# Four instead of three gate groups by seven block products, with their additions in two pieces and all feature-major weights in even chunks

## The chip, the cores and the metric

The kernel runs on one core of a Trainium2 chip. The metric is the device time of one execution in microseconds (us), lower is better. Runs of the kernel before lie between 2510.75 and 2514.31 us, and their median is 2512.1 us. The profile is of one more execution.

## The reference, cut to what matters

Two layers of a decoder trunk are computed for 256 rows (SEQ) of width 2048 (D_MODEL), all in float32:

```
h = rms_norm(x, norm_g[l]);  proj = h @ w_in[l]
(pv, pz, cq, ckv, kr, mz, cb, cc, cx, cz, xq, xz, gpre) = split(proj)
y_pool = pool_mixer(pv) * silu(pz)          # branch 0, width 1024
y_mla  = mla_mixer(cq, ckv, kr) * silu(mz)  # branch 1
y_conv = conv_mixer(cb, cc, cx) * silu(cz)  # branch 2
y_mem  = memory_xattn(xq) * silu(xz)        # branch 3
gates  = sigmoid(gpre + gate_b[l])          # 4 x 2048 columns
merged = sum over b of gates[:, b] * (y_b @ w_branch[l, b])
x = x + merged @ w_out[l]
```

The change concerns `gpre`: 256 rows by 8192 columns with an inner length of 2048, the largest part of the input projection.

## The kernel before, in words

**Products.** Every matrix product is made of TensorE matmuls over tiles of 128 (inner) by 128 by up to 512. To keep float32 accuracy, each operand is split into a high part (`hi`, made by ScalarE with a casting copy) and the rest (`lo`, made by VectorE with a subtraction), and three matmuls are summed: hi·hi, hi·lo, lo·hi. Weights are streamed once from DRAM: `wchunks` (L311) issues a load of 128x1024 numbers on SyncE's queue (`raw`, 4 buffers, L320), then the ScalarE copy (`hi`, 5 buffers, L321) and the VectorE subtraction (`lo`, 5 buffers, L322). Those three are given a priority some instructions ahead of their place (`lead`), so that weights are ready early; how early is limited by the buffers.

**Three ways to multiply.** `tm_block` (L326) makes 256 rows by 512 columns in two PSUM banks: for each of 16 inner tiles and 2 row halves the three matmuls of L334, L335, L336, so 96 matmuls of 512 columns for an inner length of 2048 and 48 for 1024. `fm_block` (L343) and `fine_block` (L372) make feature-major results of 256 or 128 features: one matmul of 512 columns (hi of the weight with hi and lo of the rows side by side) and one of 256 columns (lo of the weight) per inner tile. `seven` (L415) makes 256 rows by 1024 gate columns by the seven products of a fast 2x2 scheme (two row halves by two halves of the inner length, on operand sums `sx` and on weight differences). Per pair of inner tiles it takes two 128x1024 loads (L447), differences on VectorE (L457, L458, L467, L468), splits (L449, L456, L466, L476 on ScalarE, L441 on VectorE), and seven products of three matmuls (L432 to L434): in all 8 x 7 x 3 = 168 matmuls of 512 columns where `tm_block` takes 192.

**PSUM.** There are eight banks: three tiles `acc` of two banks and two tiles `ms` of one. A group of `seven` holds all three `acc` and one `ms` for its whole length. At its end come seven additions that gather the banks (ScalarE copy L485, VectorE L486 to L492), after which the banks are free, then the bias (a load `gb` on SyncE's queue, L496; VectorE L497), the sigmoid on ScalarE (L498) and a store to DRAM (`kept`, L499, on GpSimd's queue).

**How groups are interleaved.** `seven` is a generator: one `next` issues one product. In the stage of the pooling and the convolution branch, whose work is 48 `fine_block`s and 8 small pool matmul blocks per layer, `pull(n)` (L358) first adds n to what is owed and then issues that many products, so that products of the groups stand between the fine blocks on TensorE. A `yield True` ends a pull: in the kernel before there is one, behind the seven additions, so that one fine block stands between the additions and the bias. A fine block has one `ms` bank to itself while a group is open, and the next one needs it back: ScalarE copies it out (`fmt`, L387) and VectorE adds its halves (L388). RATE is (56 x 3 - 8) / 46 = 3.48 products per fine block. `SEVEN` lists three groups per layer: all columns of the pool branch's gates and the first half of the convolution branch's. Their gates are loaded again (`gates`, L971, `g<-kept` on GpSimd's queue) in the gate stages; the other ten blocks of 512 gate columns per layer are made there by `tm_block`.

**Order.** The order of instructions on each engine is set by a scheduler at build time, from the priorities and from the program's order; each engine then runs its list strictly in that order, and SyncE's list of loads as well.

Of the kernel before, what the change touches and what calls it, by code (L numbers as in the profile page):

```python
# [14 lines left out]
ALU = mybir.AluOpType  # L15
AX = mybir.AxisListType

P = 128
AHEAD = 100
NEAR = 40  # L20
PB = 2
D_H, D_MEM, D_LAT, D_XQ, D_MT = 4, 4, 6, 4, 3
SEQUENCE = "A0 A1 F T0 F T1 S0 A2 F V0 T2 S1 A3 F V1 T3 S2 F V2 S3 F V3 X0 X1 F Y0 Y1 X2 X3 F Y2 Y3"
CK = 2
SCRATCH = 1024
FINE = ("pv", "pz", "cc", "cx", "cb", "cz")
D = 2048
S = 256
DEPTH = 2
SEVEN = [(0, 0), (0, 1), (2, 0)]  # L30
RATE = (56 * len(SEVEN) - 8) / 46
KT = D // P
EPS = 1e-6
WINDOWS = (2, 4, 8, 16)
OFF = {
    "pv": 0, "pz": 1024, "cq": 2048, "ckv": 2560, "kr": 3072, "mz": 3136, "cb": 4160,
    "cc": 5184, "cx": 6208, "cz": 7232, "xq": 8256, "xz": 9280, "gate": 10304,
}
# [27 lines left out]
def weight_plan():  # L66
    plan, off = {}, 0

    def add(name, c0, n, nk, kt):
        nonlocal off  # L70
        plan[name, c0] = (off, n, nk, kt)
        off += P * kt * n

    def fm(name):
        if name in FINE:
            for b in range(8):
                add("in", OFF[name] + 128 * b, 128, 8, KT)
        else:
            for b in range(4):
                add("in", OFF[name] + 256 * b, 256, 4, KT)  # L80

    for e in range(4):
        add("mem_kv", 512 * e, 512, 2, KT)
    add("in", OFF["cq"], 512, 2, KT)
    for b in range(2):
        add("in", OFF["ckv"] + 288 * b, 288, 2, KT)
    for b in range(2):
        add("in", OFF["xq"] + 512 * b, 512, 2, KT)
    for hp in range(4):
        add("uq", 384 * hp, 384, 2, 4)  # L90
        add("ukv", 512 * hp, 512, 2, 4)
    for name in ("mz", "xz", "pv", "pz", "cc", "cx", "cb", "cz"):
        fm(name)
    for b in range(2):
        add("pool", 512 * b, 256, 4, 4)
    for bi in range(4):
        for e in range(4):
            if (bi, e // 2) not in SEVEN:
                add("in", OFF["gate"] + bi * D + 512 * e, 512, 2, KT)
            elif e % 2 == 0:  # L100
                add("in", OFF["gate"] + bi * D + 512 * e, 1024, 1, KT)
            add(f"br{bi}", 512 * e, 512, 2, 8)
    for e in range(4):
        add("out", 512 * e, 512, 2, KT)
    return plan, off
# [17 lines left out]
def tile_hybrid_trunk(  # L123
# [3 lines left out]
    V, A, T = nc.vector, nc.scalar, nc.tensor  # L127
# [180 lines left out]
    stream, owed, lead = [], [0.0], [AHEAD]  # L308
# [31 lines left out]
        T.matmul(ps[:, j, :], hi[:, k, n0 : n0 + P], o[:, half].rearrange("p a s -> p (a s)"), start=first, stop=False)  # L340
        T.matmul(ps[:, j, :S], lo[:, k, n0 : n0 + P], o[:, half, 0, :], start=False, stop=last)

    def fm_block(rhs, l, name, c0):  # L343
        ps = acc()
        for k0, nk, kt, n, hi, lo in wchunks(l, name, c0):
            for j in range(2):
                n0 = j * P
                for k in range(nk):
                    o = rhs[(k0 + k) // 2][:, k % 2].rearrange("p a s -> p (a s)")
                    T.matmul(ps[:, j, :], hi[:, k, n0 : n0 + P], o, start=k0 + k == 0, stop=False)  # L350
                for k in range(nk):
                    o = rhs[(k0 + k) // 2][:, k % 2, 0, :]
                    T.matmul(ps[:, j, :S], lo[:, k, n0 : n0 + P], o, start=False, stop=k0 + k == kt - 1)  # L353
        return ps


    def pull(n):
        owed[0] += n  # L358
        while stream and owed[0] >= 1:
            owed[0] -= 1  # L360
            done = next(stream[0], None)
            if done is None:
                stream.pop(0)
            if done:
                break
# [7 lines left out]
    def fine_block(rhs, l, c0):  # L373
        pull(RATE)
        ps = ms()
        for k0, nk, kt, n, hi, lo in wchunks(l, "in", c0):
            for k in range(nk):
                o = rhs[(k0 + k) // 2][:, k % 2].rearrange("p a s -> p (a s)")
                T.matmul(ps, hi[:, k, :], o, start=k0 + k == 0, stop=False)  # L379
            for k in range(nk):  # L380
                o = rhs[(k0 + k) // 2][:, k % 2, 0, :]
                T.matmul(ps[:, :S], lo[:, k, :], o, start=False, stop=k0 + k == kt - 1)  # L382
        return ps

    def fine_sum(dst, ps):
# [29 lines left out]
    def seven(l, bi, ep, h, sx):  # L415
        c0 = bi * D + 1024 * ep
# [3 lines left out]
        left, right = slice(0, 512), slice(512, 1024)  # L420
# [62 lines left out]
        c, u3 = t2("c"), t2("u3")  # L483
# [2 lines left out]
        V.tensor_tensor(g[0][:, 0, :], c, bank[2], ALU.add)  # L486
        V.tensor_tensor(c, c, bank[6], ALU.add)
        V.tensor_tensor(u3, c, bank[7], ALU.add)
        V.tensor_tensor(g[1][:, 1, :], u3, bank[5], ALU.add)
        V.tensor_tensor(c, c, bank[5], ALU.add)  # L490
        V.tensor_tensor(g[1][:, 0, :], c, bank[3], ALU.add)
        V.tensor_tensor(g[0][:, 1, :], u3, bank[4], ALU.subtract)  # L492
        yield True
        for i in range(2):
            gb = tp.tile([P, 512], F32, tag="gb", name=nm("gb"), bufs=2)
# [156 lines left out]
        return kT, vv  # L652

    def silu_half(z, i, h, l, c0):
        ps = fm_block(h, l, "in", c0 + 256 * i)
        sl = slice(2 * i, 2 * i + 2)
        fm_sum(z[:, sl, :], ps)
        sg = t2("sg").rearrange("p (n s) -> p n s", n=2)
        A.activation(sg, z[:, sl, :], AF.Sigmoid)
        V.tensor_tensor(z[:, sl, :], z[:, sl, :], sg, ALU.mult)  # L660
# [502 lines left out]
```

## Time and profile before

| what | value |
|---|---|
| median of 3 runs | 2512.1 us (2510.75 to 2514.31) |
| the profiled execution, time / span | 2505.73 us / 2504.0 us |
| TensorE busy | 2473.0 us, 12258 matmuls |
| VectorE busy / ScalarE busy | 1790.1 us / 1356.9 us |
| pool and convolution stage, layer 0 | 629 to 1031 us |
| pool and convolution stage, layer 1 | 1876 to 2277 us |
| read from HBM | 496.76 MB |

The profile's page gives busy times per engine; a busy time is the union of the instructions' own spans. TensorE's matmuls overlap in time (each row lasts longer than the distance to the next start), so what a matmul costs is read from the distance of starts, or from a count over a stretch. "PE" is TensorE, "DVE" VectorE, "ACT" ScalarE, "SP" SyncE, "POOL" GpSimd. In the view of waits, "A <- B: us, times, longest" says how long A's engine sat idle until B ended the wait. In the view of stretches, each engine has its busy time and the number of its instructions, then the granted TensorE clock, and the share and rate of the DMA engines.

### The profile page before, as it was taken

What the parts mean: (1) busy time and instruction counts of PE and PEld (TensorE: products, weight loads), DVE (VectorE), ACT (ScalarE), POOL (GpSimd) and SP (SyncE); (2) the same over time, 40 slices, a digit from 0 to 9 for tenths busy, and PEclk for the clock granted to TensorE, in tenths of its full rate; (3) what the DMA queues carried; (4) which work ended last, traced back from release to release, by engine and by line L of the source; (5) the groups of instructions that cost most, each with busy time, mean ns of one, the idle gap of its engine ahead of it and who ended that gap; (6) DMA issues with size and microseconds to landing.
All of it is one profiled execution on the core that took longest, in us unless ns stands there. A gap on an engine that the chain in (4) does not pass through costs nothing.

```text
span 2504.0 us, 33197 instructions
## 1 busy us (share of the span) xinstructions
PE 2473.0 (99%) x12258; PEld 2080.0 (83%) x12258; DVE 1790.1 (71%) x2646; ACT 1356.9 (54%) x1881; POOL 40.4 (2%) x88
## 2 busy tenths in 40 slices
PE   8999999999999999999999999999999999999999
PEld 7888888888887888888888888888888878888887
DVE  6766787555898888766474677875558888888653
ACT  7556674444565555445454566744445655555442
POOL 0000000000000000100000000000000000001000
PEclk9999999999999999999999999999999999999999
DMA  8664436677555666886655654366766556668764
GB/s 315 218 205 160 149 127 211 213 237 234 185 198 198 201 217 204 299 291 231 219 186 163 205 164 148 124 219 219 225 222 209 193 191 199 217 217 307 246 228 144
DMA packets 154052, 522.03 MB, mean 208 GB/s; under 512 B 17312, under 2 KB 18336, under 8 KB 153888
## 3 DMA queue, kind: packets, MB, share of 16 engines
q1 hardware_dynamic: 142800, 481.06, 58.2%
q0 software_dynamic: 10368, 37.75, 4.2%
q8 instruction: 96, 1.57, 0.3%
q10 hardware_dynamic: 720, 1.09, 0.1%
q14 instruction: 68, 0.56, 0.1%
HBM read 496.76 MB, written 23.07 MB: 208 GB/s over the span
## 4 chain that ended last, share of the span: by engine, by line
PE 84%; DVE 7%; DMA 5%; ACT 2%; issue 1%; SPq 0%; DVEq 0%; ACTq 0%
PE acc L336 18%; PE acc L335 18%; PE acc L334 18%; PE ms L379 10%; DMA raw<-in_weights_dram 5%; PE ms L382 5%; PE acc L350 4%; PE acc L353 2%; DVE lo L322 2%; PE acc L433 2%; PE acc L432 2%; PE acc L434 2%; DVE lo L441 1%; ACT hi L321 1%; PE ms L873 1%
## 5 line engine op out<-in xcount | busy, mean ns | idle before, releaser
L322 DVE TENSOR_TENSOR lo<-raw,hi 128x1024 fp32r<-128x1024 f32 (+1 forms) x788 | 943.3, 1199 | 578.3 <-ACT hi L321 576.1
L321 ACT CAST hi<-raw 128x1024 fp32r<-128x1024 f32 (+1 forms) x788 | 813.1, 1033 | 900.0 <-PE acc L336 568.0
L334 PE MATMUL acc<-hi,op 128*128 128x512 f32 (+2 forms) x2112 | 812.6, 385 | 5.8 <-ACT op L558 5.8
L335 PE MATMUL acc<-lo,op 128*128 128x512 f32 (+2 forms) x2112 | 808.4, 383 | 1.9 <-DVE lo L322 1.8
L336 PE MATMUL acc<-hi,op 128*128 128x512 f32 (+2 forms) x2112 | 808.9, 383 | 0.0
L334 PEld LDWEIGHTS acc<-hi,op 128*128 128x128 f32 x2112 | 397.1, 188 | 79.4 <-ACT op L558 6.4
L335 PEld LDWEIGHTS acc<-lo,op 128*128 128x128 f32 x2112 | 397.2, 188 | 77.3 <-DVE lo L322 3.5
L336 PEld LDWEIGHTS acc<-hi,op 128*128 128x128 f32 x2112 | 396.8, 188 | 76.9 <-issue 1.3
L379 PE MATMUL ms<-op,hi 128*128 128x512 f32 x1536 | 384.9, 392 | 6.7 <-ACT fmt L387 4.8
L379 PEld LDWEIGHTS ms<-op,hi 128*128 128x128 f32 x1536 | 280.8, 188 | 68.2 <-ACT fmt L387 12.3
L441 DVE TENSOR_TENSOR lo<-raw,hi 128x512 fp32r<-128x512 f32 x192 | 206.3, 1088 | 28.2 <-ACT hi L449 12.8
L382 PEld LDWEIGHTS ms<-op,lo 128*128 128x128 f32 x1536 | 209.5, 190 | 15.0
L382 PE MATMUL ms<-op,lo 128*128 128x256 f32 x1536 | 214.1, 282 | 0.0
L350 PE MATMUL acc<-op,hi 128*128 128x512 f32 x512 | 144.3, 397 | 0.0
L350 PEld LDWEIGHTS acc<-op,hi 128*128 128x128 f32 x512 | 87.6, 189 | 11.7 <-issue 0.7
L353 PEld LDWEIGHTS acc<-op,lo 128*128 128x128 f32 x512 | 78.5, 189 | 10.7 <-issue 0.7
L353 PE MATMUL acc<-op,lo 128*128 128x256 f32 x512 | 83.8, 283 | 0.0
L433 PE MATMUL acc<-lo,sx 128*128 128x512 f32 x192 | 76.4, 398 | 6.5 <-DVE lo L441 6.5
L432 PE MATMUL acc<-hi,sx 128*128 128x512 f32 x192 | 75.5, 393 | 1.0 <-ACT hi L476 1.0
L434 PE MATMUL acc<-hi,sx 128*128 128x512 f32 x192 | 74.8, 390 | 0.0
L387 ACT COPY fmt<-ms 128x512 f32<-128x512 f32 x112 | 65.0, 580 | 6.3 <-PE ms L382 5.9
L456 ACT CAST hi<-raw 128x1024 fp32r<-128x1024 f32 x48 | 50.4, 1051 | 33.1 <-DMA raw<-in_weights_dram 15.4
(254 smaller groups left out, 1985.4 us busy)
## 6 DMA issues: line engine op xcount, KB each, us to landing
raw<-in_weights_dram SPq DMA_DIRECT2D x836, 512.0 KB, 4.3
sums<-g POOLq DMA_DIRECT2D x24, 512.0 KB, 4.5
mg<-sums POOLq DMA_DIRECT2D x24, 512.0 KB, 8.1
raw<-in_weights_dram SPq DMA_DIRECT2D x32, 288.0 KB, 2.8
gb<-in_gate_b_dram SPq DMA_DIRECT2D x32, 256.0 KB, 4.4
raw<-in_weights_dram SPq DMA_DIRECT2D x16, 384.0 KB, 3.0
kept<-g POOLq DMA_DIRECT2D x12, 512.0 KB, 6.5
g<-kept POOLq DMA_DIRECT2D x12, 512.0 KB, 6.6
```

What stands on the lines that cost most here:

```text
L321: A.copy(hi[:, :m], raw[:, :m])
L322: V.tensor_tensor(lo[:, :m], raw[:, :m], hi[:, :m].bitcast(F32), ALU.subtract)
L334: T.matmul(ps[:, t, :n], hh, hi[:, k, :], start=kk == 0, stop=False)
L335: T.matmul(ps[:, t, :n], hh, lo[:, k, :], start=False, stop=False)
L336: T.matmul(ps[:, t, :n], hl, hi[:, k, :], start=False, stop=kk == kt - 1)
L350: T.matmul(ps[:, j, :], hi[:, k, n0 : n0 + P], o, start=k0 + k == 0, stop=False)
L353: T.matmul(ps[:, j, :S], lo[:, k, n0 : n0 + P], o, start=False, stop=k0 + k == kt - 1)
L379: T.matmul(ps, hi[:, k, :], o, start=k0 + k == 0, stop=False)
L382: T.matmul(ps[:, :S], lo[:, k, :], o, start=False, stop=k0 + k == kt - 1)
L432: T.matmul(bank[i], lh[0], hi[:, cols], start=u == 0, stop=False)
L433: T.matmul(bank[i], lh[0], lo[:, cols], start=False, stop=False)
L441: V.tensor_tensor(x[1][:, cols], raw[:, cols], x[0][:, cols].bitcast(F32), ALU.subtract)
```

## The change

Four things change together:

- `SEVEN` gets a fourth group, `(2, 1)`: the second half of the convolution branch's gates is made in the pool and convolution stage, too, and the two blocks of `tm_block` for it in the last gate stage go. `RATE` becomes (56 x 4 - 8) / 44 = 4.91.
- `pull` issues at most `MOST` = 6 products.
- The additions of a group come in two pieces with a `yield True` after each: first the four that fill `g[0]` and free the `ms` bank, then the three for `g[1]`. Two fine blocks (or small pool blocks) stand between the last product and the bias.
- `mz` and `xz` are packed as `pv`, `pz` and the others were: eight blocks of 128 columns in chunks of 8 inner tiles by 128 columns, where it was four blocks of 256 columns in chunks of 4 by 256. `fm_block` runs one feature tile after the other. Loads have the same size and number.

```
-SEVEN = [(0, 0), (0, 1), (2, 0)]
-RATE = (56 * len(SEVEN) - 8) / 46
+SEVEN = [(0, 0), (0, 1), (2, 0), (2, 1)]
+RATE = (56 * len(SEVEN) - 8) / 44
+MOST = 6
...
     def pull(n):
         owed[0] += n
-        while stream and owed[0] >= 1:
+        left = MOST
+        while stream and owed[0] >= 1 and left:
             owed[0] -= 1
+            left -= 1
...
         V.tensor_tensor(u3, c, bank[7], ALU.add)
+        V.tensor_tensor(g[0][:, 1, :], u3, bank[4], ALU.subtract)
+        yield True
         V.tensor_tensor(g[1][:, 1, :], u3, bank[5], ALU.add)
         V.tensor_tensor(c, c, bank[5], ALU.add)
         V.tensor_tensor(g[1][:, 0, :], c, bank[3], ALU.add)
-        V.tensor_tensor(g[0][:, 1, :], u3, bank[4], ALU.subtract)
         yield True
...
+    def fm_run(ps, rhs, l, c0):
+        for k0, nk, kt, n, hi, lo in wchunks(l, "in", c0):
+            for k in range(nk):
                o = rhs[(k0 + k) // 2][:, k % 2].rearrange("p a s -> p (a s)")
                T.matmul(ps, hi[:, k, :], o, start=k0 + k == 0, stop=False)
            for k in range(nk):
                o = rhs[(k0 + k) // 2][:, k % 2, 0, :]
                T.matmul(ps[:, :S], lo[:, k, :], o, start=False, stop=k0 + k == kt - 1)
...
+    def fm_block(rhs, l, c0):
+        ps = acc()
+        for j in range(2):
+            fm_run(ps[:, j, :], rhs, l, c0 + P * j)
+        return ps
```

**TensorE at the end of the first group, layer 0.** Before, the group's last product (into the bank `ms1064`) is followed by a whole fine block (`ms1298`, 32 matmuls, of which the rows that differ only in the inner tile are printed together):

```order
L432 MATMUL ms1064_5746<-hi1292_6876,op154_788 128x512
L433 MATMUL ms1064_5746<-lo1293_6877,op154_788 128x512
L434 MATMUL ms1064_5746<-hi1292_6876,op154_788 128x512
L379 MATMUL ms1298_6898<-op110_573,hi1300_6900 128x512 x2
L379 MATMUL ms1298_6898<-op124_632,hi1300_6900 128x512 x2
L379 MATMUL ms1298_6898<-op129_658,hi1300_6900 128x512 x2
```

Now the same product stands among the small pool blocks (`ms1257`, `ms1263`, four matmuls each), and the next group's first matmul (`acc1275`) comes right behind the second of them (rows that repeat are left out):

```order
L425 MATMUL ms1064_5748<-hi1255_6687,op154_790 128x512
L336 MATMUL ms1257_6694<-op1082_5833,hi1252_6681 128x512
L337 MATMUL ms1257_6694<-op1082_5833,lo1253_6682 128x256
L426 MATMUL ms1064_5748<-lo1256_6688,op154_790 128x512
L427 MATMUL ms1064_5748<-hi1255_6687,op154_790 128x512
L336 MATMUL ms1263_6714<-op1082_5833,hi1252_6681 128x512
L337 MATMUL ms1263_6714<-op1082_5833,lo1253_6682 128x256
L425 MATMUL acc1275_6763<-hi1281_6771,op110_575 128x512
```

The end of the first group has moved from between two fine blocks into the small pool blocks of the branch's first half. The second and third group's ends are followed by two fine blocks in a row, the fourth's by the stage's last two.

**SyncE's list of loads at the same place.** Before, the bias loads of the second group (`gb1549`, `gb1550`) stand behind the weights of that group's first pair of inner tiles (`raw1319`, `raw1320`) and one fine block's (`raw1340`, `raw1343`), and ahead of the second pair's:

```order
L447 DMA raw1319_6978<-in_weights_dram 128x1024
L447 DMA raw1320_6979<-in_weights_dram 128x1024
L320 DMA raw1340_7057<-in_weights_dram 128x1024
L320 DMA raw1343_7079<-in_weights_dram 128x1024
L496 DMA gb1549_8189<-in_gate_b_dram 128x512
L496 DMA gb1550_8194<-in_gate_b_dram 128x512
L447 DMA raw1347_7107<-in_weights_dram 128x1024
L447 DMA raw1348_7108<-in_weights_dram 128x1024
```

Now the second pair's weights stand ahead of them, and a fine block's behind:

```order
L440 DMA raw1279_6767<-in_weights_dram 128x1024
L440 DMA raw1280_6768<-in_weights_dram 128x1024
L316 DMA raw1288_6800<-in_weights_dram 128x1024
L316 DMA raw1291_6822<-in_weights_dram 128x1024
L440 DMA raw1297_6860<-in_weights_dram 128x1024
L440 DMA raw1298_6861<-in_weights_dram 128x1024
L490 DMA gb1479_7789<-in_gate_b_dram 128x512
L490 DMA gb1480_7794<-in_gate_b_dram 128x512
L316 DMA raw1304_6881<-in_weights_dram 128x1024
```

The bias loads still stand among the next group's weights, and now three times per layer, one pair of weight loads later than before.

More of the change, by code (lines that the diff above doesn't have):

```diff
@@ L25 @@
 SCRATCH = 1024
-FINE = ("pv", "pz", "cc", "cx", "cb", "cz")
 D = 2048
@@ L74, in fm @@
     def fm(name):
[L75 to L80, printed above, removed]
+        for b in range(8):
+            add("in", OFF[name] + 128 * b, 128, 8, KT)
     for e in range(4):
@@ L341, in fm_tile @@
         T.matmul(ps[:, j, :S], lo[:, k, n0 : n0 + P], o[:, half, 0, :], start=False, stop=last)
-    def fm_block(rhs, l, name, c0):
-        ps = acc()
[L345 to L353, printed above, removed]
+    def fm_run(ps, rhs, l, c0):
+        for k0, nk, kt, n, hi, lo in wchunks(l, "in", c0):
+            for k in range(nk):
+                o = rhs[(k0 + k) // 2][:, k % 2].rearrange("p a s -> p (a s)")
+                T.matmul(ps, hi[:, k, :], o, start=k0 + k == 0, stop=False)
+            for k in range(nk):
+                o = rhs[(k0 + k) // 2][:, k % 2, 0, :]
+                T.matmul(ps[:, :S], lo[:, k, :], o, start=False, stop=k0 + k == kt - 1)
+    def fm_block(rhs, l, c0):
+        ps = acc()
+        for j in range(2):
+            fm_run(ps[:, j, :], rhs, l, c0 + P * j)
         return ps
@@ L375, in fine_block @@
         ps = ms()
[L376 to L382, printed above, removed]
+        fm_run(ps, rhs, l, c0)
         return ps
@@ L654, in silu_half @@
     def silu_half(z, i, h, l, c0):
-        ps = fm_block(h, l, "in", c0 + 256 * i)
+        ps = fm_block(h, l, c0 + 256 * i)
         sl = slice(2 * i, 2 * i + 2)
```

## The prediction

> **What bounds the kernel now.** I read the page first. TensorE is busy in 99% of the span; VectorE, which makes the low parts of all weights, in 71%.
>
> ```profile
> span 2504.0 us, 33197 instructions
> PE 2473.0 (99%) x12258; PEld 2080.0 (83%) x12258; DVE 1790.1 (71%) x2646; ACT 1356.9 (54%) x1881; POOL 40.4 (2%) x88
> ```
>
> An average hides the stages, so I asked next for four stretches: the pool and convolution stage of layer 0, what follows it, a stretch of the gate stage of layer 1, and the pool and convolution stage of layer 1.
>
> ```profile
> core 0: us, PE busy (x) PEld busy (x) DVE busy (x) ACT busy (x) POOL busy (x), PEclk, DMA share, GB/s
> 629.00:1031.00 402.00, 392.94 (x2075) 334.21 (x2074) 348.94 (x447) 232.33 (x275) 4.83 (x13) 1.00 0.62 205
> 1031.00:1119.00 88.00, 87.39 (x395) 72.04 (x394) 59.67 (x57) 37.78 (x41) 9.14 (x17) 1.00 0.86 317
> 1660.00:1860.00 200.00, 200.00 (x884) 165.65 (x883) 107.19 (x89) 83.66 (x80) 5.51 (x11) 1.00 0.71 228
> 1876.00:2277.00 401.00, 392.75 (x2073) 334.17 (x2072) 348.28 (x445) 233.34 (x275) 4.84 (x13) 1.00 0.62 205
> ```
>
> In the gate stage TensorE never waits and VectorE is half idle (107 of 200 us). In the stage where the groups are interleaved it is the other way: VectorE is busy 348.9 of 402 us (0.868), and TensorE is idle for 402.0 - 392.9 = 9.1 us in layer 0 and 8.2 us in layer 1. The change moves work from the first kind of stage into the second. What TensorE waits for there, in layer 0:
>
> ```profile
> engine line waited for: us in total, times, longest us
> PE acc L433 <- DVE lo L441: 3.3, 3, 1.6
> PE ms L379 <- ACT fmt L387: 2.6, 4, 1.4
> PE ms L379 <- ACT hi L321: 1.4, 1, 1.4
> PE ms L340 <- ACT fmt L387: 1.2, 1, 1.2
> ```
>
> The rest is one wait of a product for ScalarE. Two kinds stand out: a product waits for the low part of its weights (L433), and a fine or small block waits for the one `ms` bank, which ScalarE has still to copy out (`fmt`). So TensorE's matmuls set the time, and the change is worth what it takes off them less what it adds to these waits.
>
> **The change part by part, for one layer.**
>
> *Gate blocks that go.* Two `tm_block`s of 96 matmuls leave the last gate stage. The gate stretch above holds 884 matmuls in 200 us without a wait, 0.2262 us each: 192 x 0.2262 = **-43.4 us**. Their 32 low parts, bias and sigmoid go with them, all hidden there.
>
> *The fourth group.* One pull of TensorE's list in layer 0, between two fine blocks:
>
> ```profile
> 839.80 1.11 PE L382 MATMUL ms<-op,lo 128*128 128x256 f32 x8
> ...
> 842.59 1.11 PE L382 MATMUL ms<-op,lo 128*128 128x256 f32 x8
> 843.55 0.40 PE L432 MATMUL ms<-hi,op 128*128 128x512 f32 x1
> ...
> 845.61 1.98 PE L379 MATMUL ms<-op,hi 128*128 128x512 f32 x8
> ```
>
> Nine product matmuls start from 843.55 to 845.61: 0.229 us each, 0.69 us a product. The group has 168: **+38.5 us**. (One chunk of a fine block, eight `lo` and eight `hi`, takes 842.59 - 839.80 = 2.79 us, a fine block 5.58.)
>
> *Even chunks.* The count of matmuls stays. In the old form, four `lo` take as long as two `hi`:
>
> ```profile
> 353.53 0.63 PE L350 MATMUL acc<-op,hi 128*128 128x512 f32 x2
> 354.00 0.63 PE L353 MATMUL acc<-op,lo 128*128 128x256 f32 x4
> 354.47 0.40 PE L350 MATMUL acc<-op,hi 128*128 128x512 f32 x1
> ```
>
> So four and four take 0.94 + 0.47 = 1.41 us, eight and eight 2.82 against 2.79. A layer has 32 of these; 0.03 x 32 = 1.0 is the most, and the last digit could make it nothing. I take **-0.5 us** (0 to -1.0). A low part is now wanted after eight matmuls, not four, which can only relax a wait.
>
> *VectorE in the stage.* These rows are of the same stage, with the mean duration behind the busy time; below them VectorE's own list at the first group's end:
>
> ```profile
> L322 DVE TENSOR_TENSOR lo<-raw,hi 128x1024 fp32r<-128x1024 f32 x100 | 121.9, 1222 | 38.3 <-ACT hi L321 37.7
> L467 DVE TENSOR_TENSOR raw<-raw,raw 128x512 f32<-128x512 f32 x24 | 16.5, 687 | 0.2
> ```
>
> ```profile
> 757.16 0.68 DVE L457 TENSOR_TENSOR raw<-raw 128x512 f32<-128x512 f32 x1
> 757.76 0.68 DVE L487 TENSOR_TENSOR c<-c,acc 128x512 f32<-128x512 f32 x1
> ...
> 763.42 1.22 DVE L497 TENSOR_TENSOR g<-g,gb 128x1024 f32<-128x1024 f32 x1
> 764.56 0.69 DVE L669 TENSOR_TENSOR z<-z,sg 128x512 f32<-128x512 f32 x1
> ```
>
> Starts lie 0.60 us apart behind an operation of 512 columns and 1.14 behind one of 1024. A group has 24 whole low parts, 8 half ones, 32 differences, 7 additions and 2 bias additions: 26 x 1.14 + 47 x 0.60 = 57.8 us, against 38.5 us that it gives TensorE. VectorE's work in the stage becomes 348.9 + 57.8 = 406.7 us, TensorE's 392.9 + 38.5 = 431.4. TensorE stays the longer, and its bare time is what counts, but VectorE's slack falls from 44 to 25 us. [...]
>
> *The limit of six products* only moves products to later pulls; no cost of its own.
>
> *The additions in two pieces, and the waits.* Where TensorE stood still, with the wait and its releaser in brackets:
>
> ```profile
> 724.44 0.50 PE L340 MATMUL ms<-op,hi 128*128 128x512 f32 x1 [1.16 <-ACT fmt L387]
> ...
> 768.17 0.50 PE L433 MATMUL acc<-lo,sx 128*128 128x512 f32 x1 [1.60 <-DVE lo L441]
> ...
> 771.62 0.50 PE L433 MATMUL acc<-lo,sx 128*128 128x512 f32 x1 [1.09 <-DVE lo L441]
> ...
> 913.78 2.11 PE L379 MATMUL ms<-op,hi 128*128 128x512 f32 x8 [1.38 <-ACT hi L321]
> ```
>
> 724 is the first small pool block while a group is open; 768 and 772 lie behind the first group's additions, 914 behind the second's. The view of waits over the whole span has both layers' waits of the first kind, and the longer one:
>
> ```profile
> PE ms L340 <- ACT fmt L387: 3.1, 2, 2.0
> ```
>
> Four things change. The small blocks of both halves of the pool branch now meet an open group's `ms` bank right behind a fine block: a second wait of the 724 kind, +1.2 to +2.0, taken +1.6. The first group's end has about 2.8 us of small blocks beside it (four, each of two matmuls of 0.229 and two of 0.12, an eighth of 843.55 - 842.59) where a fine block gave 5.58; its additions must free `acc` first: -1 to +4, taken +0.5, since the waits at 768 and 772 that it replaces fall away. A third end between groups is added, at the price of the 914 row: +1.4 (0 to 2.7). And pulls of five or six products last 3.4 to 4.1 us where three last 2.1, so ScalarE's copy of the `ms` bank is no longer late: of the 2.6 us, -2.0 (0 to -2.6). Together **+1.5 us**; the bounds, -1 to +5, are narrower than the sum of the ends since these waits share VectorE's backlog.
>
> *Behind the stage.* Six blocks of 48 branch matmuls in a row become eight, with gates and sums reloaded beside the weights. In 1031 to 1119 the DMA engines are busy 0.86 of the time and TensorE lost 88.00 - 87.39 = 0.6 us. The two added blocks want less (no sum is stored there): **+0.3 us** (0 to 0.8).
>
> Sum per layer: -43.4 + 38.5 - 0.5 + 1.5 + 0.3 = -3.6; twice, **-7.2 us**. The profiled execution (2505.73 us, 1.7 around its span) would be at 2498.5; it stands 6.4 below the runs' median, to which I apply the same sum: **2504.9 us**.
>
> [...]
>
> **The rivals.**
>
> *VectorE sets the pace (slower).* The busiest 100 us that I found for it:
>
> ```profile
> 660.00:760.00 100.00, 98.34 (x521) 83.95 (x520) 90.00 (x120) 60.85 (x74) 0.13 (x1) 1.00 0.57 195
> ```
>
> If 0.90 is all that it can hold, since it also waits for ScalarE's casts (37.7 us in the L322 row), the stage takes 406.7 / 0.90 = 451.9 us, +49.9: per layer -43.4 + 49.9 - 0.5 + 0.3 = +6.3, in all 2524.7. It decides from where the share cannot pass 406.7 / 445.6 = 0.913 (402.0 + 43.4 + 0.5 - 0.3 = 445.6). My forecast needs 406.7 / 442 = 0.92, more than any row shows. Against it: what holds back the casts in this stage is largely TensorE, which has not yet released the buffers:
>
> ```profile
> ACT hi L321 <- PE ms L379: 45.2, 34, 1.7
> ```
>
> The supply thus has some 45 us of room, and the group takes 57.8 - 38.5 = 19.3 of it. Chance 0.17.
>
> *The bias loads hold up the weights (no change).* SyncE's list at the first group's end:
>
> ```profile
> 752.50 3.12 SPq L320 DMA_DIRECT2D raw<-in_weights_dram  x2
> 764.67 2.07 SPq L496 DMA_DIRECT2D gb<-in_gate_b_dram  x2
> 768.18 3.74 SPq L447 DMA_DIRECT2D raw<-in_weights_dram  x2
> ```
>
> SyncE stands for 9.0 us until the first bias addition (763.42 + 1.22) frees a `gb` buffer, and the weights queued behind, for fine blocks and for products, come late. The second piece puts the bias one block later still, up to 5.58 us. If each of three ends then costs the two product waits that followed here (1.60 and 1.09, 2.7), where one does today, that is +5.4 in place of +1.5: per layer +0.3, in all 2512.7. For it: the row. Against: one more pair of weights now stands ahead of the bias loads. Chance 0.20.
>
> *The waits go (faster than forecast).* If two fine blocks beside the additions and the longer pulls remove all but about 4 us of the 9.1 us idle, that is -5.0 in place of +1.5: per layer -10.1, in all 2491.9. Against it: the first group's end has small blocks beside it. Chance 0.15.
>
> *That the fourth group is not interleaved* is excluded: 47 pulls of 4.91 and 8 of 1 make 239 steps, four groups need 4 x 58 = 232, and in TensorE's new list the last product stands ahead of the stage's last two fine blocks.
>
> **How the numbers follow.** The forecast's own case has 0.48; by its waits it reaches from 2 x (-43.4 + 38.5 - 0.5 - 1 + 0.3) = -12.2 to -0.2, so 2499.9 to 2511.9. A change under 0.2% (5.0 us) is about what a measurement of this kernel cannot tell from none. Faster by more: the waits go, 0.15, some three quarters of the forecast's case, 0.37, and 0.02 of the bias loads; 0.54. Within: 0.11 of the forecast and 0.16 of the bias loads; 0.27. Slower: VectorE 0.17 and 0.02 of the bias loads; 0.19. The range leaves out about half of the case in which the waits go and most of VectorE's: 2493 to 2519.
>
> **What would show it.** In the changed profile, the pool and convolution stage should last about 442 us with VectorE busy about 407; the gate stage behind it should be shorter by 43 us; waits for `fmt` ahead of fine blocks should be fewer and those of products at group ends should show VectorE's `lo`. The prediction is wrong if the stage exceeds 446 us, or if TensorE's idle time in it falls under 5 us.

## The result, and the profile after

The changed kernel takes 2538.51 us (median of 4 runs, 2536.42 to 2539.46) where the kernel before takes 2511.69 us beside it (4 runs): a ratio of 1.0115, with a 95% interval of 1.0103 to 1.0127. It is slower, and outside the predicted range. The profiled execution took 2536.42 us, its span 2534.1 us, 30.1 more than before. (The medians lie 26.8 us apart; the profiled execution of the kernel before, 2505.73 us, was shorter than its other runs.)

The page of the changed kernel: TensorE is busy 8.0 us longer than before although it runs 48 matmuls fewer, in a span that is 30.1 us longer, and VectorE is busy 75.8 us longer.

```profile
span 2534.1 us, 33322 instructions
PE 2481.0 (98%) x12210; PEld 2080.2 (82%) x12210; DVE 1865.9 (74%) x2756; ACT 1379.8 (54%) x1915; POOL 44.6 (2%) x96
```

The lengths of the stages, read as the distance from each stage's first matmul to the next one's (the third row up to the first matmul behind the stage's last fine block):

| stage | before | after | forecast per layer |
|---|---|---|---|
| attention, layer 0 and 1 | 160.0, 160.0 | 159.0, 159.0 | -0.5 with the next row |
| gate blocks behind it | 255.7, 255.7 | 256.2, 256.2 | |
| pool and convolution, layer 0 and 1 | 401.8, 401.0 | 461.5, 460.8 | +40.0 |
| what follows, to the next attention or the end | 429.0, 227.1 | 383.6, 182.3 | -43.1 |

The loss is all in one stage: 59.7 us more per layer where 40.0 were forecast. Of these, 1.2 us are not a loss: in the changed kernel five matmuls of the next stage's first gate block (L330 to L332) run ahead of the stage's last fine block, and the fourth row is shorter by as much.

```profile
1085.50 0.40 PE L330 MATMUL acc<-hi,op 128*128 128x512 f32 x1
...
1086.43 0.39 PE L331 MATMUL acc<-lo,op 128*128 128x512 f32 x1
1086.66 1.98 PE L343 MATMUL ms<-op,hi 128*128 128x512 f32 x8
```

These are the stretches of the changed kernel: the pool and convolution stage of both layers, then what follows the first, and the first 80 us of it alone. The columns are those of the prediction's stretches.

```profile
630.70:1092.20 461.50, 440.99 (x2246) 370.80 (x2245) 410.36 (x522) 262.74 (x310) 5.89 (x15) 0.98 0.61 201
1891.00:2351.80 460.80, 440.99 (x2247) 371.12 (x2246) 410.21 (x522) 263.10 (x310) 5.89 (x15) 0.98 0.61 201
1092.20:1475.80 383.60, 383.60 (x1837) 323.13 (x1836) 239.66 (x355) 200.72 (x312) 10.23 (x19) 1.00 0.68 229
1092.20:1172.00 79.80, 79.80 (x362) 66.06 (x361) 56.69 (x53) 35.31 (x38) 10.23 (x19) 1.00 0.96 360
```

VectorE is busy 410.4 us, the forecast's 407. TensorE is idle for 461.5 - 441.0 = 20.5 us where it was 9.1, and its busy time is 441.0 where 392.9 + 38.5 = 431.4 was forecast. The granted clock, 1.00 before, has fallen to 0.98. The DMA engines move 201 GB/s here, and 360 GB/s in the 80 us behind the stage, so the transfers themselves are not at their limit. TensorE's waits in the stage of layer 0:

```profile
PE ms L343 <- ACT fmt L380: 6.9, 8, 1.5
PE ms L336 <- ACT fmt L380: 3.5, 3, 2.1
PE acc L425 <- DVE c L480: 3.1, 1, 3.1
PE acc L426 <- DVE lo L434: 2.7, 3, 1.5
PE ms L343 <- ACT hi L317: 1.3, 3, 0.4
```

Against the rows of before, the waits for the copy out of the `ms` bank (`fmt`) have grown from 2.6 + 1.2 to 6.9 + 3.5 us, where I had let them shrink. The wait for VectorE's `c` is the first group's end among the small pool blocks. ScalarE, which makes those copies and the high parts, waits in this stage of the changed kernel for:

```profile
ACT hi L317 <- DMA raw<-in_weights_dram: 51.3, 44, 4.4
ACT hi L469 <- DVE raw L461: 32.1, 15, 5.9
ACT hi L449 <- DMA raw<-in_weights_dram: 25.1, 17, 2.1
ACT hi L459 <- DVE raw L451: 14.4, 11, 3.4
ACT hi L317 <- PE ms L343: 13.1, 11, 1.7
ACT hi L442 <- DMA raw<-in_weights_dram: 12.9, 15, 2.2
```

And in the same stage of the kernel before, which the prediction did not quote except for the second row:

```profile
ACT hi L321 <- DMA raw<-in_weights_dram: 54.8, 37, 4.0
ACT hi L321 <- PE ms L379: 45.2, 34, 1.7
ACT hi L449 <- DMA raw<-in_weights_dram: 14.2, 11, 2.1
ACT hi L456 <- DMA raw<-in_weights_dram: 7.6, 7, 2.2
ACT hi L476 <- DVE raw L468: 6.4, 5, 2.8
ACT hi L466 <- DVE raw L458: 4.1, 3, 1.5
```

The room, casts that wait for TensorE, has gone from 45.2 to 13.1 us, and casts now wait for loads for 89.3 us (51.3 + 25.1 + 12.9). They had already waited 76.6 us for loads before (54.8 + 14.2 + 7.6). What grew most is another wait: casts that wait for VectorE's differences of the weights, from 10.5 us (6.4 + 4.1) to 46.5 (32.1 + 14.4). One wait for a load and what came of it, first ScalarE's list of the changed kernel, then SyncE's, VectorE's and TensorE's:

```profile
1015.34 0.61 ACT L442 CAST hi<-raw 128x512 fp32r<-128x512 f32 x1
1020.28 1.04 ACT L317 CAST hi<-raw 128x1024 fp32r<-128x1024 f32 x1 [4.33 <-DMA raw<-in_weights_dram]
1021.23 0.58 ACT L380 COPY fmt<-ms 128x512 f32<-128x512 f32 x1
```

```profile
1015.43 7.51 SPq L316 DMA_DIRECT2D raw<-in_weights_dram  x3
```

```profile
1014.19 1.22 DVE L434 TENSOR_TENSOR lo<-raw,hi 128x1024 fp32r<-128x1024 f32 x1
```

```profile
1015.22 1.12 PE L346 MATMUL ms<-op,lo 128*128 128x256 f32 x8
1016.17 0.40 PE L425 MATMUL acc<-hi,op 128*128 128x512 f32 x1
...
1020.05 0.39 PE L427 MATMUL acc<-hi,op 128*128 128x512 f32 x1
1021.87 2.11 PE L343 MATMUL ms<-op,hi 128*128 128x512 f32 x8 [1.43 <-ACT fmt L380]
```

Read it backwards. TensorE waits 1.43 us for the `ms` bank. The fine block in that bank ended at about 1016.2, six products ago, but its copy (`fmt`, 1021.23) stands in ScalarE's list behind a cast that waits 4.33 us for its load. SyncE issued that load at 1015.43, just when VectorE's low part ended (1014.19 + 1.22 = 1015.41) and with it the use of a `raw` buffer. So a buffer that came free late made a load late, the load a cast, and the cast a copy that had nothing to do with it.

### The profile page after: what moved, and what is told of

Same layout as the page of the kernel before. It is cut to its first block, busy times and chain, and to the rows that moved or that the text cites. A ratio compares the mean times of both kernels' runs of the same rounds, so it can differ in the third digit from the quotient of the medians.

```text
span 2534.1 us, 33322 instructions
## 1 busy us (share of the span) xinstructions
PE 2481.0 (98%) x12210; PEld 2080.2 (82%) x12210; DVE 1865.9 (74%) x2756; ACT 1379.8 (54%) x1915; POOL 44.6 (2%) x96
## 5 line engine op out<-in xcount | busy, mean ns | idle before, releaser
L318 DVE TENSOR_TENSOR lo<-raw,hi 128x1024 fp32r<-128x1024 f32 (+2 forms) x756 | 903.1, 1197 | 525.2 <-ACT hi L317 523.4
L317 ACT CAST hi<-raw 128x1024 fp32r<-128x1024 f32 (+2 forms) x756 | 777.6, 1032 | 785.4 <-PE acc L332 527.4
L330 PE MATMUL acc<-hi,op 128*128 128x512 f32 (+2 forms) x1984 | 763.9, 385 | 6.0 <-ACT op L552 5.7
L331 PE MATMUL acc<-lo,op 128*128 128x512 f32 (+2 forms) x1984 | 758.9, 382 | 1.4 <-DVE lo L318 1.3
L332 PE MATMUL acc<-hi,op 128*128 128x512 f32 (+2 forms) x1984 | 759.1, 383 | 0.0
L330 PEld LDWEIGHTS acc<-hi,op 128*128 128x128 f32 x1984 | 373.3, 188 | 75.7 <-ACT op L552 6.4
L331 PEld LDWEIGHTS acc<-lo,op 128*128 128x128 f32 x1984 | 373.5, 188 | 71.7 <-DVE lo L318 2.5
L332 PEld LDWEIGHTS acc<-hi,op 128*128 128x128 f32 x1984 | 373.0, 188 | 71.3 <-DVE op L553 0.7
L343 PE MATMUL ms<-op,hi 128*128 128x512 f32 x1536 | 390.7, 396 | 17.0 <-ACT fmt L380 13.6
L343 PEld LDWEIGHTS ms<-op,hi 128*128 128x128 f32 x1536 | 283.0, 190 | 81.5 <-ACT fmt L380 21.0
L434 DVE TENSOR_TENSOR lo<-raw,hi 128x1024 fp32r<-128x1024 f32 (+1 forms) x256 | 274.6, 1087 | 32.6 <-ACT hi L469 15.5
L346 PEld LDWEIGHTS ms<-op,lo 128*128 128x128 f32 x1536 | 210.5, 191 | 15.4
L343 PE MATMUL acc<-op,hi 128*128 128x512 f32 x512 | 134.9, 397 | 0.0
L426 PE MATMUL acc<-lo,sx 128*128 128x512 f32 x256 | 102.4, 400 | 6.0 <-DVE lo L434 5.7
L449 ACT CAST hi<-raw 128x1024 fp32r<-128x1024 f32 x64 | 67.3, 1052 | 71.4 <-DMA raw<-in_weights_dram 56.9
L425 PE MATMUL acc<-hi,sx 128*128 128x512 f32 x256 | 101.6, 397 | 4.1 <-ACT hi L459 2.5
L469 ACT CAST hi<-raw 128x1024 fp32r<-128x1024 f32 x64 | 67.2, 1051 | 67.4 <-DVE raw L461 61.4
L343 PEld LDWEIGHTS acc<-op,hi 128*128 128x128 f32 x512 | 90.6, 189 | 16.2 <-issue 1.3
L427 PE MATMUL acc<-hi,sx 128*128 128x512 f32 x256 | 100.7, 394 | 0.0
L459 ACT CAST hi<-raw 128x1024 fp32r<-128x1024 f32 x64 | 67.2, 1050 | 37.1 <-DVE raw L451 26.1
```

The costliest lines, as they stand in the source:

```text
L317: A.copy(hi[:, :m], raw[:, :m])
L318: V.tensor_tensor(lo[:, :m], raw[:, :m], hi[:, :m].bitcast(F32), ALU.subtract)
L330: T.matmul(ps[:, t, :n], hh, hi[:, k, :], start=kk == 0, stop=False)
L331: T.matmul(ps[:, t, :n], hh, lo[:, k, :], start=False, stop=False)
L332: T.matmul(ps[:, t, :n], hl, hi[:, k, :], start=False, stop=kk == kt - 1)
L425: T.matmul(bank[i], lh[0], hi[:, cols], start=u == 0, stop=False)
```

## The experiments

The theories at the start: VectorE's work sets the pace (theory A in the expectations); the four `raw` buffers do not free themselves fast enough for two streams of weights (theory B); the first group's end among the small blocks halves the clock (theory C); the bias loads hold up the weights. In the table, "stage" is the pool and convolution stage of layer 0 and 1, and the ratio is to the kernel before on the same chip. The stages of e3, e4, e6, e7 and e10 contain 1.2 us of the next stage as well, that of e8 0.5 us. e6, e13 and e15 leave out a part of the computation.

| kernel | time, us | ratio, 95% interval | stage, us |
|---|---|---|---|
| e1_chunks | 2504.85 | 0.9993 (0.9983 to 1.0002) | 401.5, 401.9 |
| e2_four_plain | 2532.46 | 1.0101 (1.0086 to 1.0116) | 458.7, 455.9 |
| e3_pieces | 2515.57 | 1.0032 (1.0020 to 1.0045) | 407.4, 408.4 |
| e8_one_piece | 2537.08 | 1.0120 (1.0105 to 1.0135) | 461.3, 460.7 |
| e4_raw5 | 2495.88 | 0.9956 (0.9942 to 0.9971) | 442.1, 440.7 |
| e5_early | 2530.54 | 1.0089 (1.0071 to 1.0107) | 457.3, 460.1 |
| e6_relief | 2522.07 | 1.0061 (1.0037 to 1.0084) | 456.2, 455.5 |
| e7_bias_pool | 2533.33 | 1.0108 (1.0090 to 1.0126) | 461.8, 459.6 |
| e9_three_raw5 | 2488.57 | 0.9929 (0.9915 to 0.9942) | 392.8, 393.5 |
| e10_trims | 2535.83 | 1.0117 (1.0101 to 1.0134) | 457.5, 458.4 |
| e11_raw5_early | 2491.53 | 0.9939 (0.9927 to 0.9952) | 441.0, 439.2 |
| e12_plain_raw5 | 2498.26 | 0.9967 (0.9954 to 0.9979) | 440.3, 441.4 |
| e13_raw5_early_relief | 2482.36 | 0.9898 (0.9884 to 0.9913) | 434.6, 434.8 |
| e14_three_raw5_chunks | 2488.78 | 0.9921 (0.9906 to 0.9935) | 392.9, 393.8 |
| e15_three_raw5_relief | 2489.97 | 0.9929 (0.9912 to 0.9945) | 393.3, 393.1 |
| e16_bias_add_pool | 2501.22 | 0.9966 (0.9955 to 0.9976) | 441.9, 445.5 |
| e17_three_raw5_again | 2488.58 | 0.9921 (0.9900 to 0.9942) | 393.9, 393.5 |

### Which part of the change loses

**The even chunks alone** (before, with `fm_run` and eight blocks of 128 columns).

> The kernel before with the even chunks alone, three groups. All theories: the attention stage, which takes 160.0 us per layer before, should lose about 1 us as it does with the whole change (159.0), so 2509 to 2512 us, and the pool and convolution stage should stay at 401 to 402 us. If the chunks were to blame for the loss, this would be slower by several us.

Attention is 1.0 us shorter per layer, the gate blocks behind it 0.5 longer: -0.5 as forecast, and no difference that the measurement can tell.

**The fourth group alone** (before, with one list entry; `RATE` follows).

```
-SEVEN = [(0, 0), (0, 1), (2, 0)]
+SEVEN = [(0, 0), (0, 1), (2, 0), (2, 1)]
```

> The kernel before with the fourth group alone: RATE is (56 x 4 - 8) / 46 = 4.70, the additions are in one piece, there is no limit of six products, and the chunks are the old ones. Theory A, VectorE's work sets the pace: its work is the same as with the whole change, the stage is again 455 to 462 us, 2532 to 2540 us in all. Theory B, weights come late because the groups hold the four raw buffers, and ScalarE's copies of the fine block's bank stand in line behind the casts: also 450 to 460 us. Theory C, the first group's end among the small pool blocks and the halved clock behind it make the loss: here the first group ends just behind the pool blocks with one fine block beside it, so no long wait and no stretch of half clock there; the stage is about 445 us and the total about 2510 us.

1.0101 of the 1.0115: the fourth group makes nearly the whole loss by itself. Its first end lies elsewhere, and the stage still takes 458.7 us where theory C expected 445, so where that end stands is not the main cause. (Stretches of half clock, shown in the last section, are not gone here: 6.8 us in layer 0 and 10.2 in layer 1, against 17.0 per layer in the whole change; the mean granted clock of the profiled execution is 0.996 here and 0.992 there. e5 below tests theory C more closely.)

**The two pieces alone** (before with the additions in two pieces and `/ 44`, three groups) **and the change with one piece**.

> The kernel before with the additions in two pieces and RATE (56 x 3 - 8) / 44 = 3.64, three groups. Theories A and B: VectorE's work and the loads are as before, so the time stays within 5 us of before (2507 to 2517 us). Theory C: the second piece leaves a wait at the first group's end among small pool blocks, 3 to 8 us per layer, more if the clock is halved behind it: 2518 to 2530 us.

> The changed kernel with the additions in one piece again, RATE 4.91, limit six, four groups. The first group still ends among the small pool blocks, one pull earlier done. Theories A and B: within 5 us of the changed kernel (2533 to 2543 us). Theory C: the waits at the ends change; if the second piece is to blame, 2515 to 2530 us.

With three groups the two pieces, with the rate that belongs to them, cost 8.5 us over the kernel before beside it (0.3%): more than the 5 us that theories A and B allow, so they have some cost of their own. With four, taking them back gains nothing (1.0120 against 1.0115).

### What the stage waits for

**A fifth `raw` buffer in the changed kernel.** Its 4 KB per partition are taken from temporaries:

```
-            raw = wp.tile([P, 1024], F32, tag="raw", name=nm("raw"), bufs=4)
+            raw = wp.tile([P, 1024], F32, tag="raw", name=nm("raw"), bufs=5)
...
-            pT = tp.tile([P, 512], F32, tag="pT", name=nm("pT"), bufs=2)
+            pT = tp.tile([P, 384], F32, tag="pT", name=nm("pT"), bufs=2)
...
-        return tp.tile([P, 512], F32, tag="t2", name=nm(s), bufs=7)
+        return tp.tile([P, 512], F32, tag="t2", name=nm(s), bufs=6)
```

(and two kinds of small tiles from 6 to 4 buffers).

> The changed kernel with five raw buffers in place of four, paid for with one t2 buffer, a narrower pT, and four small buffers in place of six. Theory A, VectorE's work sets the pace: the stage shortens by at most 3 us per layer from 461. Theory B, late weights in the four raw buffers hold up ScalarE's list: weights come earlier, ScalarE's waits for loads in the stage (about 90 us per layer) fall by a third or more, and the stage shortens by 8 us or more per layer. Theory C: the long wait at the first group's end stays, the stage is shorter by under 5 us.

The stage falls by 19.4 and 20.1 us, with VectorE's work where it was. These are its stretches, TensorE's waits and ScalarE's in layer 0:

```profile
629.40:1071.50 442.10, 433.91 (x2247) 369.76 (x2246) 408.29 (x522) 261.79 (x310) 5.89 (x15) 0.99 0.64 210
```

```profile
PE ms L336 <- ACT fmt L380: 2.8, 2, 2.5
PE acc L425 <- DVE c L480: 2.3, 1, 2.3
PE acc L426 <- DVE lo L434: 1.4, 1, 1.4
```

```profile
ACT hi L459 <- DVE raw L451: 35.2, 16, 3.5
ACT hi L317 <- PE ms L343: 33.8, 26, 2.1
ACT hi L469 <- DVE raw L461: 23.3, 8, 4.8
ACT hi L317 <- DMA raw<-in_weights_dram: 13.3, 11, 2.4
```

The waits of fine blocks (`L343`) for `fmt` are gone; ScalarE's waits of this kind (L317) for loads fell from 51.3 to 13.3 us, and its waits for TensorE rose from 13.1 to 33.8: the room is back. With the loads of the groups (L449, L442) its waits for loads fell from 89.3 to 18.9 us.

**The control: the same temporaries cut, `raw` at four.**

> The changed kernel with the smaller t2, pT and small pools alone, and four raw buffers: the control for the run with five. Theory B: no gain, 2533 to 2545 us. If the scheduler's new order under other pools, and not the fifth buffer, made the gain, it is near 2496 us.

1.0117, as without the cut. (Its profiled execution, 2529.93 us, was one of its shorter ones, with stages of 457.5 and 458.4 us.) Against that profile the fifth buffer still takes 15.4 and 17.7 us off the stage.

**The first end moved** (the owed count starts one pull higher).

```
-        owed[0] = -RATE
+        owed[0] = RATE
```

> The changed kernel with what is owed starting at +RATE in place of -RATE: the first group ends in the last two fine blocks ahead of the first half's small pool blocks, not among them. Theory C: the wait of 3 us and the 10 us of half clock behind it go, 8 to 12 us per layer, so 2514 to 2524 us. Theories A and B: the work of the stage is the same, what is saved there is lost elsewhere: 2530 to 2542 us.

The half clock falls from 17.0 to 3.4 and 6.8 us per layer (the mean granted clock of the profiled execution is 0.998 against 0.992), and the stage hardly moves (457.3, 460.1): with late weights, what is saved there is lost elsewhere in the stage. Theory C falls as the main cause.

**Work taken off VectorE**: the window sums of the pooling and the taps of the convolution are left out.

```
-                while sh < w:
+                while sh < 1:
...
-                V.tensor_scalar(y[:, n, :], u[:, n, 0:S], w[0], None, ALU.mult)
-                V.scalar_tensor_tensor(y[:, n, :], u[:, n, 1 : S + 1], w[1], y[:, n, :], ALU.mult, ALU.add)
-                V.scalar_tensor_tensor(y[:, n, :], u[:, n, 2 : S + 2], w[2], y[:, n, :], ALU.mult, ALU.add)
```

> The changed kernel without the taps of the convolution and the window sums of the pool branch on VectorE (left out, so the two branches' values are others): about 19 us of VectorE's 410 us per layer go, while loads, casts and TensorE's work stay. Theory A: the stage shortens by 15 to 21 us per layer, to about 442. Theory B: it shortens by 0 to 6 us. Theory C: by 0 to 6 us.

VectorE's busy time falls by 12.7 us, to 397.7 (the 19 us of the expectation were too many), the stage by 5.3. Theory A falls as the main cause while the buffers are short: here ScalarE's waits for loads even rose, to 104.5 us.

**The groups' bias loads on GpSimd's queue.**

```
-            nc.sync.dma_start(gb, bcast_rows(gate_b[l, c0 + 512 * i : c0 + 512 * (i + 1)]))
+            nc.gpsimd.dma_start(gb, bcast_rows(gate_b[l, c0 + 512 * i : c0 + 512 * (i + 1)]))
```

> The changed kernel with the groups' bias loads issued on GpSimd's queue, so that SyncE's list of weight loads no longer stands behind a bias load that waits for its buffer (11 us of such waits in layer 0's stage). If that list's stops are to blame, the stage shortens by 3 to 8 us per layer; theory A: by under 2 us; theory B: by 1 to 5 us.

The stage stays (461.8, 459.6). That rival is out.

### Does the fourth group pay with the weights on time?

**Three groups with a fifth buffer** (e9: the kernel before with the edit of e4), and four groups with it in two more forms: with the first end moved (e11: the edits of e4 and e5) and without the pieces and chunks (e12: e2 with the edit of e4).

> The kernel before, three groups, with the fifth raw buffer and the same smaller pools that paid for it. Theory B (the four raw buffers are what the fourth group overloads): with three groups the buffers nearly suffice, so the stage shortens by 2 to 8 us per layer, 2492 to 2504 us in all. If the fifth buffer gave as much here as with four groups (20 us per layer), the fourth group would not be what overloads them, and this would be at 2470 us.

> Four groups with five raw buffers, and the first group's end ahead of the small pool blocks. With five buffers that end still costs two waits of 2.5 us and 6.8 us of half clock in each layer. Theory C for what is left: both go, 6 to 8 us per layer, 2480 to 2485 us. If what is saved there is lost elsewhere as with four buffers: 2492 to 2498 us.

> The fourth group alone (one piece, no limit, old chunks, RATE 4.70) with five raw buffers. Theory B: the loss goes as in the whole change, 2490 to 2500 us. The two pieces and the limit are worth something once the weights are on time if this is slower than 2496 us by more than 3; nothing or less if it is at or under 2496.

The kernel before gains as well, 9.0 and 7.5 us per stage, where 2 to 8 were expected, and at 2488.6 us it is ahead of all with four groups (2491.5 to 2498.3). Of e11 it is ahead by 3 us only, and the intervals of the two ratios overlap. The smaller pools with four buffers were run only with four groups (e10), so for three groups the gain is not parted from theirs. e12 lies between the two bounds of its expectation, and what the pieces and the limit are worth stays open. The stretch of e9, and all that TensorE waits for there:

```profile
628.60:1021.40 392.80, 390.01 (x2073) 334.56 (x2072) 348.08 (x446) 233.86 (x275) 4.83 (x13) 1.00 0.62 210
```

```profile
PE acc L433 <- DVE lo L441: 2.7, 2, 1.6
```

So with five buffers the fourth group costs 441.0 - 392.8 = 48.2 and 439.2 - 393.5 = 45.7 us where it saves some 44 behind the stage: still 8.5 above its 38.5 of work. The pairs that differ in the list entry alone and the rate that follows say how much the buffers explain: with four buffers the group costs 458.7 - 401.8 = 56.9 and 455.9 - 401.0 = 54.9 us (e2), with five 440.3 - 392.8 = 47.5 and 441.4 - 393.5 = 47.9 (e12 against e9). So the fifth buffer takes away about half of what the group costs beyond its work.

**VectorE again, now with five buffers**, with four groups (e13: e11 with the edit of e6) and as a control with three (e15: e9 with it).

> The four groups with a fifth raw buffer and the early start of the pulls (stage 441.0 and 439.2 us, VectorE busy 407), without the convolution's taps and the pooling's window sums, which are left out of the computation (some 13 us of VectorE's work per layer). Theory: with the weights on time it is VectorE that keeps TensorE waiting, so the stage shrinks by 8 us or more per layer (432 or less) and the time to about 2475. Rival: the buffers are still the limit, so the stage shrinks by 3 us at most, ScalarE's waits for loads grow, and the time is 2486 or more.

> The control: three groups with a fifth raw buffer, without the same VectorE work (convolution's taps and window sums left out of the computation). VectorE is busy 348 of 393 us there and TensorE idle only 2.8 us. Theory (VectorE is what the fourth group meets): little to gain, 1 to 3 us per layer, clearly less than with four groups. Rival (the relief helps by shortening a chain that both kernels have): as much as with four groups.

```profile
627.50:1062.10 434.60, 430.95 (x2241) 365.66 (x2240) 395.45 (x488) 263.56 (x312) 7.23 (x15) 1.00 0.66 218
```

Four groups gain 6.4 and 4.4 us per layer, three gain nothing (393.3, 393.1 against 392.8, 393.5). Neither number of the expectation was met, but the two together tell: behind the buffers it is VectorE's work that the fourth group meets, for some 5 of the 8.5 us. What makes up the other 3 is open.

**Relief with nothing left out**: the groups' bias additions on GpSimd, in the kernel of e11.

```
-            V.tensor_tensor(g[i], g[i], gb.unsqueeze(1).broadcast_to([P, 2, 512]), ALU.add)
+            nc.gpsimd.tensor_tensor(g[i], g[i], gb.unsqueeze(1).broadcast_to([P, 2, 512]), ALU.add)
```

> The four groups with a fifth raw buffer and the early start of the pulls, the eight bias additions per layer (1.22 us each, 9.7 us of VectorE's work) moved to GpSimd. Theory: VectorE's work is what the fourth group still meets, so the stage shrinks by 3 to 5 us per layer from 441.0 and 439.2, and the time falls to about 2484. Rival: an addition on GpSimd is slower and holds the bias buffer and SyncE's queue behind it longer, or disturbs VectorE; then the stage stays at 440 or grows.

> The three-group kernel with a fifth raw buffer once more, on the same chip as the kernel beside it: ratio to the kernel before 0.993. If the fourth group pays once VectorE is relieved, this is the slower of the two.

The rival won: the stage grew to 441.9 and 445.5, and the kernel takes 2501.22 us beside 2488.58 us for three groups on the same chip. Both of its ways show. SyncE's list stood for 21.8 us in layer 0's stage until an addition on GpSimd gave a bias buffer back, where it was 8.1 us in e11, and VectorE was disturbed; no run parts the two. One place, GpSimd's list and VectorE's:

```profile
735.92 2.43 POOL L491 TENSOR_TENSOR g<-g,gb 128x1024 f32<-128x1024 f32 x1
```

```profile
734.82 0.67 DVE L486 TENSOR_TENSOR g<-c,acc 128x512 f32<-128x512 f32 x1
735.42 0.68 DVE L460 TENSOR_TENSOR raw<-raw,raw 128x512 f32<-128x512 f32 x1
736.02 3.41 DVE L434 TENSOR_TENSOR lo<-raw,hi 128x1024 fp32r<-128x1024 f32 x1
```

The low part beside the addition takes 3.41 us instead of 1.22.

**The best of both**: three groups, five buffers, even chunks.

> Three groups as before, with a fifth raw buffer and the even chunks. The two parts lie in different stages: attention -1.0 us per layer, pool and convolution stage 393 as with the fifth buffer alone. About 2486.5, the fastest so far.

2488.78 us: the chunks add nothing that can be told. The version to keep is the kernel before with a fifth `raw` buffer.

## Why the prediction was wrong, point by point

- **Gate blocks that go and the DMA behind the stage** (-43.4 + 0.3): measured 383.6 - 429.0 = -45.4 and 182.3 - 227.1 = -44.8, of which 1.2 us are the five matmuls that moved into the stage ahead. Right to about 1 us.
- **The fourth group's matmuls** (+38.5): right as work. With most waits gone (e13 against e15) the stage differs by 434.7 - 393.2 = 41.5 us, waits included.
- **Even chunks** (-0.5): right (-1.0 + 0.5).
- **VectorE's work** (406.7): right to 4 us, 410.4 and, with the early start and five buffers, 407.4.
- **The waits** (+1.5, bounds -1 to +5): this is the step that failed. TensorE's idle time rose by 20.5 - 9.1 = 11.4 us, and its busy time by 9.6 more than the products explain; together with the 38.5 that is 59.5 of the 59.7 (of the 9.6 about 6.5 are half clock, see below, and 1.2 the five matmuls of the next stage). I priced each wait by a like one in the trace of before and took the supply of weights as given. The ground was the 45.2 us of casts that wait for TensorE, which I called room for the group's 19.3. But the same view's first row, 54.8 us of casts that wait for loads, was left unread: for part of the stage ScalarE already had no weights in hand. A pair of a group holds two of the four `raw` buffers through a round of differences and splits, and the stage now has 32 such rounds where it had 24. e4 with its control e10 shows that a fifth buffer takes 15 to 20 us off the stage. Since three groups gain some 8 us by it as well, it explains about half of what the fourth group costs beyond its products (e2, e12 and e9); some 5 us more are VectorE's work (e13, e15), and some 3 are open. The two causes hang together, since a `raw` buffer is free only when VectorE has made the low part from it.
- **"ScalarE's copy of the `ms` bank is no longer late" (-2.0)**: of the opposite sign: the waits for `fmt`, small blocks included, grew by 6.6 us. I had looked at TensorE's side alone, where longer pulls give the copy more time, and not at what stands ahead of the copy on ScalarE.
- **The clock** (no term): one was missing. The clock was halved for 10.2 + 3.4 + 3.4 us per layer, of which 7.1 + 3.4 + 3.4 us were matmuls. Matmuls of 512 columns started (750.29 - 747.73) / 6 = 0.427 us apart there and 0.227 apart at full clock, so nearly half of such time is loss: 13.9 x (1 - 0.227 / 0.427) = 6.5 us of the 9.6 went there, an estimate. I gave it no term because PEclk was 1.00 in every stretch of before that the prediction shows; what stood ahead of the halved clock in the changed kernel is in the last section.
- **The rivals.** The slower one named VectorE, with 2524.7 us. Its mechanism is not what made most of the loss: with 12.7 us less of VectorE's work the stage was 5.3 us shorter (e6), and with five buffers VectorE does the same 408 us of work in a stage of 442, above the 0.90 that I had given as its possible limit (408.3 / 442.1 = 0.92). It is what is late next. The bias loads cost nothing that shows (e7). The rival by which the waits go had the sign wrong.
- **The saving itself.** Even without any new wait the sum was -43.6 + 38.5 per layer, some 5 us. A gain that is a small difference of two large terms has no cover: a stage of 440 us that comes out 1.2% longer turns its sign.

## What to carry to other kernels

Before work is moved into a stage that streams weights, count for how long each load buffer is held and read what the casting engine waits for: if it waits for loads while the DMA engines are far from busy (here 89.3 us at a share of 0.61), suspect the number of buffers, and try one more. Here the cast that waited 4.33 us for its load delayed the copy behind it in ScalarE's list, and TensorE waited 1.43 us for that copy, so it may pay to keep a copy that frees a bank from standing behind a cast whose weights are late; no run here tried that order. And try the extra buffer on the kernel before the change as well: here it was worth 0.7% by itself, and the change nothing beside it.

## What the runs showed of the hardware that was not expected

**The clock fell behind waits of under 1 us, too.** Stretches of the changed kernel with the granted clock in the third column from the end, and TensorE ahead of the last:

```profile
740.50:750.70 10.20, 7.14 (x20) 5.50 (x19) 10.16 (x18) 5.33 (x8) 0.00 (x0) 0.50 0.31 104
880.50:883.90 3.40, 3.40 (x13) 2.92 (x12) 2.71 (x4) 2.04 (x3) 0.11 (x1) 0.50 0.86 300
1034.10:1037.50 3.40, 3.40 (x10) 2.72 (x9) 3.33 (x6) 1.50 (x2) 0.00 (x0) 0.50 0.80 284
```

```profile
1030.51 0.39 PE L427 MATMUL acc<-hi,sx 128*128 128x512 f32 x1
1031.70 0.49 PE L425 MATMUL acc<-hi,sx 128*128 128x512 f32 x1 [0.81 <-ACT hi L469]
1032.96 0.50 PE L426 MATMUL acc<-lo,sx 128*128 128x512 f32 x1 [0.77 <-DVE lo L434]
```

In the 3.4 us ahead of 1034.1 no wait is longer than 0.81 us; by the distances of starts TensorE stood still for about (1031.70 - 1030.51 - 0.23) + (1032.96 - 1031.70 - 0.23) = 2.0 us of them, and half clock followed for one stretch of 3.4 us. At the first group's end it lasted 10.2 us, three times as long: a wait of 2.08 us ended just ahead of that stretch, and one of 3.06 us fell into it. The trace's own record of the granted clock gives the lengths: in both stages the stretches at 0.50 last 3.413 us or 10.240, and those at 1.00 between them 129.706, 150.186 and 962.558 us, which is 38, 44 and 282 times 3.4133. If the two stages are cut into stretches of 3.413 us in step with these, and a matmul is counted with its distance of starts (0.227 us for 512 columns, 0.118 for 256), matmuls fill 0.27 to 0.41 of the six stretches at full clock behind which the clock is halved, and 0.43 or more of every other one at full clock; the shares are estimates from the starts in the trace. So the clock was halved behind the six emptiest stretches of the two stages; 0.41 and 0.43 lie close together, and no run tested what decides.

**An addition on GpSimd held up VectorE.** In e16 the 2.43 us addition and a low part started together, and the low part ended 739.43 - 738.35 = 1.08 us behind the addition's end, about its own 1.22 us, as if it had stood still until then. VectorE's busy time in the stage was 413.5 us against 407.4 in e11, although 9.7 us of work had left it. What made it stand still is not shown.
